# A two-layer network on one core: v and y by groups in DRAM, ScalarE's queue for v, and the side work of the last gate product dealt out over its rows

## The chip, the core and the metric

One core of a Trainium2 chip runs the whole program in one launch. The metric is the device time of an execution in microseconds (us), as the median of several executions.

## What is computed

Two layers over 512 tokens and a model width of 2048, in fp32. Layer 0 (forgetting attention beside an RWKV-7 mix) is untouched by the change. Layer 1 and the end that both layers share are, cut to what matters:

```python
def chunked_spatial_gating(u, v, ln_g, ln_b, w_s, b_s):      # chunks of 128 tokens, 16 groups of 128 channels
    u = gelu(u)
    v = layer_norm(gelu(v), ln_g, ln_b)
    vc = v.reshape(B, T // 128, 128, 16, 128)
    mixed = einsum('gts,bnsgc->bntgc', w_s * causal, vc) + b_s.T[:, :, None]
    return u * mixed.reshape(B, T, 2048)

xn = rms_norm(h, norm_pre[1])
u, v, g = split(xn @ c_w_in, 3)                              # 2048 x 6144
oc = chunked_spatial_gating(u, v, c_ln_g, c_ln_b, c_w_s, c_b_s)
y = (oc * silu(g)) @ c_w_out                                 # 2048 x 2048
h = h + rms_norm(y, norm_post[1])
h = h + (p[1] @ ple_w_proj[1]) * sigmoid(h @ ple_w_gate[1])  # the last gate product, 2048 x 2048
```

## The kernel before

**Products.** Every fp32 product is made of three matmuls of halves: an operand is cast to a rounded high part (`hi`, by ScalarE) and the rest is its low part (`lo`, VectorE subtracts); then hi*hi, hi*lo and lo*hi are added in PSUM. Weights come by DMA into `raw` or `rq` buffers; `pieces` casts them to `whi` (L1352, ScalarE) and `wlo` (L1353, VectorE), with four buffers each.

**Seven products.** The two large products of the change, `xn @ c_w_in` and `h @ ple_w_gate`, are computed by the scheme of seven block products in place of eight (`seven`, matmuls at L1380 to L1382). The tokens are halved (256 and 256), the contraction is halved (channel tiles 0 to 7 and 8 to 15), and a pair of 512-column blocks is taken at a time. The left operands are *sets* of blocks: set 1 is the block of the first half and the first tokens (`A11`), set 2 the one of the second half (`x2`), set 4 the block of the second half and the later tokens (`set22`), and sets 5, 6, 3 and 7 are sums and differences of blocks (S1, S2, S4 and S3 in `sets`, at L1243, L1246, L1249 and L1252). Each block of a set is split into hi and lo by `finish` (L959 ScalarE, L960 VectorE). For some of the products the weights are differences too: GpSimd loads a second block on top of the first with an accumulating DMA (L1309), or VectorE adds (L1313). A product is 8 rows of 6 matmuls (128x128 by 128x512).

**Side work.** After each row `seven` calls `tick()`; `later(n, step)` hangs a step n rows ahead. The steps are written into the program at that row, and a scheduler then sets each engine's order from the program's order, dependencies and priorities. So the places in the code are a request, and the order of each engine is to be read from the engine's own list.

**Layer C (layer 1).** The columns of v come first: `vals` applies gelu and stores v in DRAM (`vd`, [128, 4, 2048]: token in chunk, chunk, channel). Then u and g follow by column pairs, the result staying in `u[n]`. `mix(g, at)` hangs four steps for each of 16 groups around a row `at`: `load` at -11 (v of the group into buffer `sq`, L1467, w_s, L1468, and two rows of the layer norm spread over partitions, L1469 and L1470, into the buffers `rstdB` or `accq`; all four on SP's queue), `norm` at -7 (four activations of ScalarE, L1476, a mask and two multiply-adds of GpSimd, L1480 and L1481), `split` at 0 (w_s transposed, both cast) and `mul` at +3 (three matmuls, L1486, and VectorE's gating of u, L1492). The first half of the result y is stored (`yd2`, L1543, on ScalarE's queue) and comes back on SP's queue at L1536 for its transposes, while the later column pairs are still computed.

**Last layer.** `post_norm` multiplies by `c_w_out`. Behind it TensorE does the small product `p @ ple_w_proj` as filler; ScalarE copies its results into `sg` (L1134) and SP stores them (`pd`, L1135). Then `update` adds the normed y to h on VectorE (L1143, L1144), first for the first 256 tokens (e = 0), later for the other half (e = 1). `A11` is split right behind its updates. `sets` then does, in one stretch of code: set 2, the updates of e = 1, and all sums. `flip(g, m)` transposes h back to token order (TensorE L1157), ScalarE copies it into `sg` (L1159) and stores it to `rd` (L1160); sixteen flips hang at rows 0 to 15, and set 4 at row 16. The gate product runs over its 14 block products; `fetch` brings `pd` and `rd` back on SP's queue (L1185, L1186) into spare buffers, and `emit` multiplies by the sigmoid, adds (L1189 to L1192) and stores the output (L1194).

Each kind of temporary buffer in the pool `wp` (`sg`, `sq`) has two buffers, so a third writer waits until the first has been read.

## Time and profile before

| | |
|---|---|
| timed, median of 2 runs | 2325.9 us (2325.39 to 2326.41) |
| the profiled execution | 2323.41 us, its span from first to last instruction 2321.7 us |
| TensorE (PE) busy | 2237.6 us, 96% of the span |
| TensorE weight loads (PEld), beside it | 79% |
| VectorE (DVE) / ScalarE (ACT) / GpSimd (POOL) | 64% / 53% / 12% |
| mean granted TensorE clock | 0.987 of full speed |
| DMA | mean 134 GB/s over the span |
| layer C, from about 1480 us on | to about 1920 us, TensorE busy 406.61 of 440 us |
| its output product | to about 2090 us, busy 170.00 of 170 us |
| filler, first rows of the last gate product | to about 2182 us, busy 67.31 of 92 us |
| the rest of it, to the end | busy 126.86 of 139 us |

How rows of the trace are read below. A window row gives its start and end, its length, TensorE's busy time with the number of matmuls, the granted clock, the mean share of 16 DMA engines and GB/s. An instruction row gives its start, its length, engine, line, operation, what it writes <- reads and its shape, how often it follows at once (x4), and in brackets the idle time ahead of it and what ended it. "SPq" and "ACTq" are the queues by which SP and ScalarE issue transfers. A group row (a line, an operation, a shape, a count) gives busy time and mean ns of one, then the idle time ahead of its instructions. A row with KB gives the count of transfers, the size of one and the median time from issue to landing. A wait row gives the sum, the count and the longest.

### The profile page before, as it was taken

How to read it: one execution, taken by the hardware profiler on the slowest of the kernel's cores; microseconds unless marked ns; L12 is line 12 of the kernel's file. 1: busy time of each engine (PE TensorE's matmuls, PEld its weight loads, DVE VectorE, ACT ScalarE, POOL GpSimd, SP SyncE). 2: the span in 40 equal slices, each digit the busy share in tenths (PEclk: the TensorE clock that was granted, in tenths of full speed). 3: DMA queues.
4: the chain of work that ended last, by engine and by line, in shares of the span. 5: the costliest groups of instructions: out<-in, count | busy, mean ns of one | idle time of the engine just before them, and what ended most of it. 6: DMA issues, size and time to landing. Idle time of an engine off the chain costs nothing.

```text
span 2321.7 us, 39023 instructions
## 1 busy us (share of the span) xinstructions
PE 2237.6 (96%) x14787; PEld 1823.7 (79%) x14787; DVE 1480.6 (64%) x2817; ACT 1229.2 (53%) x2510; POOL 284.8 (12%) x334
## 2 busy tenths in 40 slices
PE   9999999999999999999999999999979989996898
PEld 7878888888887888878888888887658768885676
DVE  8666657766535878852365469877766764228668
ACT  5455555555444777743354357565545643336544
POOL 2000101010100000001100011122330220010010
PEclk9999999999999999999999999999999989999899
DMA  6332223222335433352335345896576764335786
GB/s 229 89 85 77 67 72 88 72 79 61 96 96 170 124 100 105 84 162 92 109 112 164 118 136 158 210 237 165 139 178 180 178 178 135 100 100 163 240 226 196
DMA packets 298969, 311.58 MB, mean 134 GB/s; under 512 B 14701, under 2 KB 198158, under 8 KB 297758
## 3 DMA queue, kind: packets, MB, share of 16 engines
q1 hardware_dynamic: 275614, 265.06, 37.7%
q0 software_dynamic: 17408, 33.56, 8.5%
q10 hardware_dynamic: 5760, 10.49, 1.2%
q8 instruction: 116, 1.90, 0.3%
q14 instruction: 71, 0.58, 0.1%
HBM read 274.15 MB, written 34.90 MB: 133 GB/s over the span
## 4 chain that ended last, share of the span: by engine, by line
PE 76%; DMA 9%; DVE 9%; ACT 3%; issue 2%; SPq 0%; POOL 0%; ACTq 0%; DVEq 0%
PE mm L195 11%; PE mm L197 11%; PE mm L196 11%; PE mm L982 6%; PE mm L983 6%; PE mm L981 6%; PE mm L1381 5%; PE mm L1382 5%; PE mm L1380 5%; DVE wlo L1353 3%; DMA sq<-vd 2%; DMA rq<-in_ple_w_gate_dram 2%; PE tm L533 1%; DMA rq<-in_c_w_in_dram 1%; PE tm L554 1%
## 5 line engine op out<-in xcount | busy, mean ns | idle before, releaser
L181 DVE TENSOR_TENSOR wlo<-raw,whi 128x512 fp32r<-128x512 f32 x464 | 331.8, 722 | 423.3 <-ACT whi L179 383.8
L179 ACT CAST whi<-raw 128x512 fp32r<-128x512 f32 x464 | 287.3, 620 | 455.9 <-PE mm L982 222.4
L196 PE MATMUL mm<-xl,whi 128*128 128x512 f32 x1088 | 426.9, 392 | 0.0
L195 PE MATMUL mm<-xh,whi 128*128 128x512 f32 x1008 | 418.1, 415 | 0.0
L197 PE MATMUL mm<-xh,wlo 128*128 128x512 f32 x1008 | 398.0, 395 | 0.0
L1353 DVE TENSOR_TENSOR wlo<-rq,whi 128x512 fp32r<-128x512 f32 x336 | 240.9, 728 | 121.2 <-ACT whi L1352 120.8
L1352 ACT CAST whi<-rq 128x512 fp32r<-128x512 f32 x336 | 206.2, 620 | 150.0 <-PE mm L1382 86.6
L196 PEld LDWEIGHTS mm<-xl,whi 128*128 128x128 f32 x1088 | 205.2, 189 | 33.6
L197 PEld LDWEIGHTS mm<-xh,wlo 128*128 128x128 f32 x1008 | 189.2, 188 | 41.8
L195 PEld LDWEIGHTS mm<-xh,whi 128*128 128x128 f32 x1008 | 189.8, 188 | 33.8
L981 PE MATMUL mm<-yl,whi 128*128 128x512 f32 x336 | 130.9, 390 | 0.0
L983 PE MATMUL mm<-yl,wlo 128*128 128x512 f32 x336 | 130.7, 389 | 0.0
L1380 PE MATMUL mm<-whi,yh 128*128 128x512 f32 x256 | 103.2, 403 | 14.8 <-ACT whi L1352 14.8
L1424 POOL TENSOR_TENSOR accq<-accq,sq 128x512 f32<-128x512 f32 x42 | 56.8, 1353 | 476.5 <-ACT sq L1422 475.4
L982 PE MATMUL mm<-xl,whi 128*128 128x512 f32 x288 | 112.0, 389 | 0.0
L1381 PE MATMUL mm<-wlo,yh 128*128 128x512 f32 x256 | 103.2, 403 | 4.2 <-DVE wlo L1353 4.2
L1381 PE MATMUL mm<-wlo,yl 128*128 128x512 f32 x256 | 101.4, 396 | 4.9 <-DVE wlo L1353 4.9
L1381 PE MATMUL mm<-wlo,xl 128*128 128x512 f32 x256 | 101.6, 397 | 4.3 <-DVE wlo L1353 4.0
L1380 PE MATMUL mm<-whi,yl 128*128 128x512 f32 x256 | 101.2, 395 | 3.5 <-ACT whi L1352 2.8
L1382 PE MATMUL mm<-whi,yh 128*128 128x512 f32 x256 | 101.9, 398 | 0.0
L1380 PE MATMUL mm<-whi,xl 128*128 128x512 f32 x256 | 101.1, 395 | 0.0
L1382 PE MATMUL mm<-whi,yl 128*128 128x512 f32 x256 | 100.7, 393 | 0.0
(486 smaller groups left out, 4701.3 us busy)
## 6 DMA issues: line engine op xcount, KB each, us to landing
raw<-in_ab_w_in_dram SPq DMA_DIRECT2D x128, 512.0 KB, 3.9
rq<-in_c_w_in_dram SPq DMA_DIRECT2D x75, 512.0 KB, 6.9
rq<-in_c_w_in_dram POOLq DMA_DIRECT2D x38, 512.0 KB, 8.5
raw<-in_ple_w_gate_dram SPq DMA_DIRECT2D x36, 512.0 KB, 3.8
rq<-in_ple_w_gate_dram SPq DMA_DIRECT2D x36, 512.0 KB, 5.1
raw<-in_ab_w_out_dram SPq DMA_DIRECT2D x32, 512.0 KB, 3.7
raw<-in_c_w_out_dram SPq DMA_DIRECT2D x32, 512.0 KB, 3.8
raw<-in_c_w_in_dram SPq DMA_DIRECT2D x25, 512.0 KB, 6.2
```

The source lines that it names most:

```text
L179: nc.scalar.copy(hi[:, : m * n], src)
L181: self.weng.tensor_tensor(lo[:, : m * n], src, f(hi[:, : m * n]), ALU.subtract)
L195: nc.tensor.matmul(acc, hi, xhi[k], start=(k == 0), stop=False)
L196: nc.tensor.matmul(acc, hi, xlo[k], start=False, stop=False)
L197: nc.tensor.matmul(acc, lo, xhi[k], start=False, stop=(k == nk - 1))
L981: nc.tensor.matmul(accs[j], hi[:, js], xhi[k], start=(k == 0), stop=False)
L982: nc.tensor.matmul(accs[j], hi[:, js], xlo[k], start=False, stop=False)
L983: nc.tensor.matmul(accs[j], lo[:, js], xhi[k], start=False, stop=(k == nk - 1))
L1353: nc.vector.tensor_tensor(lo, src, f(hi), ALU.subtract)
L1380: nc.tensor.matmul(acc[m], xh, hi, start=(first and r == 0), stop=False, **more)
L1381: nc.tensor.matmul(acc[m], xh, lo, start=False, stop=False, **more)
L1382: nc.tensor.matmul(acc[m], xl, hi, start=False, stop=(r == 7), **more)
```

## The change

v and the first half of y are kept in DRAM by groups of 128 channels, so that what a group needs lies together: `vd` is [128, 16, 4, 128] and `yd2` [128, 8, 4, 128]. Stores are scattered into rows of 512 bytes, loads read 2 KB in one piece per partition. The four loads of a group's `load` go out by ScalarE's queue instead of SP's; `norm` hangs at -5 instead of -7 and `mul` at +4 instead of +3. y is loaded eight rows instead of five ahead of its transposes, which hang one to three rows later. The stores of `pd` go out by ScalarE's queue, from `sg` and `sq` in turn.

In the last layer the stretch `sets` becomes closures of one q each (`sums`), and these and the flips are hung at rows: flips of the first tokens at 1 to 8, the updates of e = 1 with set 5 at 2, 6, 10 and 14, sets 6 and 3 at 19 to 28 (which form the difference `less` a second time), flips of the later tokens at 20 to 34, set 7 at 37 to 40, set 4 at 42. The first fetches go into the eight `yh` buffers that set 7 takes over later, and from row 46 on into the former spares. For layer 1's other call of the sums the order is the same as before, since it runs them at once.

```diff
-            self.vd, self.pd, self.rd = (self.t(dp, [P, 4, D], n) for n in ("vd", "pd", "rd"))
-            self.yd2 = self.t(dp, [P, 4, 2 * T], "yd2")
+            self.pd, self.rd = (self.t(dp, [P, 4, D], n) for n in ("pd", "rd"))
+            self.vd, self.yd2 = (self.t(dp, [P, c, 4, P], n) for n, c in (("vd", KT), ("yd2", 8)))
...
                 for m in range(4):
-                    pj = self.t(wp, [P, T], "sg")
+                    pj = self.t(wp, [P, T], ("sg", "sq")[m % 2])
                     nc.scalar.copy(pj, accs[m])
-                    nc.sync.dma_start(self.pd[:, m, g * T : (g + 1) * T], pj)
+                    nc.scalar.dma_start(self.pd[:, m, g * T : (g + 1) * T], pj)
...
+        sets, x2, less, s1, s24, s3 = self.sums(H, wp)
+        sets[1] = A11
+        for q in range(4):
+            x2(q)
+        spare = [[], []]
         def late(q):
             update(q, 1)
             update(q + 4, 1)
-        sets = self.sets(A11, H, ps, wp, None, False, late)
+            s1(q)
...
+        def early_spare():
+            for j in range(8):
+                spare[j % 2].append(self.slot("yh", j, F32))
+        def late_spare():
             for j in range(2):
                 tl = self.t(self.xp, [P, 4, T], f"xh{2 + j}")
-                spare.append([tl[:, q, :] for q in range(4)])
-        for k, (g, m) in enumerate((g, m) for g in (2, 0, 3, 1) for m in range(4)):
-            self.later(k, lambda g=g, m=m: flip(g, m))
-        self.later(16, rest)
+                spare[j][:] = [tl[:, q, :] for q in range(4)]
+        def x22():
+            sets[4] = self.set22(H, wp, False)
+        steps = [(1 + k, lambda g=g, m=m: flip(g, m)) for k, (g, m) in enumerate((g, m) for g in (2, 0, 3, 1) for m in (0, 1))]
+        steps += [(2 + 4 * q, lambda q=q: late(q)) for q in range(4)]
+        steps += [(16, early_spare)]
+        steps += [(19 + 3 * q, lambda q=q: s24(q, less(q))) for q in range(4)]
+        steps += [(20 + 2 * k, lambda g=g, m=m: flip(g, m)) for k, (g, m) in enumerate((g, m) for g in (2, 0, 3, 1) for m in (2, 3))]
+        steps += [(37 + q, lambda q=q: s3(q)) for q in range(4)]
+        steps += [(42, x22), (46, late_spare)]
+        for n, step in steps:
+            self.later(n, step)
...
+    def sums(self, xs, wp):
...
+        def x2(q):
+            self.part(s[2], q, xs[q + 4, 0])
+        def less(q):
+            t = self.tmp(wp, "sg")
             nc.vector.tensor_tensor(t, xs[q, 1], xs[q + 4, 1], ALU.subtract)
...
+        def s1(q):
+            t = less(q)
+            self.part(s[5], q, t)
+            return t
+        def s24(q, t):
+            u = self.tmp(wp, "sq")
             nc.vector.scalar_tensor_tensor(u, t, -1.0, xs[q, 0], ALU.mult, ALU.subtract)
+            self.part(s[6], q, u)
+            t = self.tmp(wp, "sg")
             nc.vector.scalar_tensor_tensor(t, u, -1.0, xs[q + 4, 0], ALU.mult, ALU.subtract)
+            self.part(s[3], q, t)
+        def s3(q):
+            t = self.tmp(wp, "sq")
             nc.vector.tensor_tensor(t, xs[q, 0], xs[q, 1], ALU.add)
...
-            nc.scalar.dma_start(self.vd[:, m, n * T : (n + 1) * T], dst)
+            nc.scalar.dma_start(self.vd[:, 4 * n : 4 * n + 4, m, :], dst.rearrange("p (g c) -> p g c", c=P))
...
-                nc.sync.dma_start(vn, self.vd[:, :, gs])
-                nc.sync.dma_start(own["ws"], i["c_w_s"][0, g])
-                nc.sync.dma_start(own["bc"][:, 0, :], i["c_ln_g"][0, gs].partition_broadcast(P))
-                nc.sync.dma_start(own["bc"][:, 1, :], i["c_ln_b"][0, gs].partition_broadcast(P))
+                nc.scalar.dma_start(vn, self.vd[:, g])
+                nc.scalar.dma_start(own["ws"], i["c_w_s"][0, g])
+                nc.scalar.dma_start(own["bc"][:, 0, :], i["c_ln_g"][0, gs].partition_broadcast(P))
+                nc.scalar.dma_start(own["bc"][:, 1, :], i["c_ln_b"][0, gs].partition_broadcast(P))
...
-            for n, step in ((-11, load), (-7, norm), (0, split), (3, mul)):
+            for n, step in ((-11, load), (-5, norm), (0, split), (4, mul)):
...
-                nc.sync.dma_start(y, self.yd2[:, :, n * P : (n + 1) * P])
-            self.later(at - 5, load)
+                nc.sync.dma_start(y, self.yd2[:, n])
+            self.later(at - 8, load)
...
-                nc.scalar.dma_start(self.yd2[:, m, n * T : (n + 1) * T], u[n][:, m, :])
+                nc.scalar.dma_start(self.yd2[:, 4 * n : 4 * n + 4, m, :], u[n][:, m, :].rearrange("p (g c) -> p g c", c=P))
...
-                    early(n, (14, 18, 22, 26, 31, 35, 39, 43)[n])
+                    early(n, (17, 21, 25, 29, 32, 36, 40, 44)[n])
```

Line numbers move with the change: L1140 and L1141 are the copy and the store of `pd`, L1149 and L1150 the update, L1163 to L1166 a flip, L1268, L1278, L1281 and L1286 the sums, L1384 and L1385 whi and wlo, L1499 to L1502 the four loads of a group, L1508 its norm, L1520 and L1523 the casts of its `split`, L1575 the store of `yd2`.

**VectorE, at the start of the last gate product.** Before, the updates of a block of h (`yh_4263`, `yh_4269`, ...: L1143, L1144) and the low parts of the first set (`xh_4492`, L960) alternate; `wlo` at L181 belongs to the products ahead.

```order
L1143 TENSOR_TENSOR xl_4260_20528<-xl_4260_20528,rstdB_12776 128x512
L1143 TENSOR_TENSOR xl_4266_20544<-xl_4266_20544,rstdB_12776 128x512
L1144 TENSOR_TENSOR yh_4263_20537<-yh_4263_20537,xl_4260_20528 128x512
L1144 TENSOR_TENSOR yh_4269_20553<-yh_4269_20553,xl_4266_20544 128x512
L181 TENSOR_TENSOR wlo_21621<-raw_21602,whi_21620 128x512
L960 TENSOR_TENSOR xh_4492_21699<-yh_4263_20537,xh_4491_21698 128x512
L960 TENSOR_TENSOR xh_4492_21699<-yh_4269_20553,xh_4491_21698 128x512
L1143 TENSOR_TENSOR xl_4316_20836<-xl_4316_20836,rstdB_12776 128x512
L1143 TENSOR_TENSOR xl_4322_20852<-xl_4322_20852,rstdB_12776 128x512
L181 TENSOR_TENSOR wlo_21655<-raw_21652,whi_21654 128x512
L1144 TENSOR_TENSOR yh_4319_20845<-yh_4319_20845,xl_4316_20836 128x512
L1144 TENSOR_TENSOR yh_4325_20861<-yh_4325_20861,xl_4322_20852 128x512
```

In the change's order the last rows ahead of those low parts are these: updates of the later tokens (`yh_4320`, `yh_4398`, `xh_4411` and so on).

```order
L1149 TENSOR_TENSOR xl_4317_20838<-xl_4317_20838,rstdB_12776 128x512
L1149 TENSOR_TENSOR yh_4398_21262<-yh_4398_21262,rstdB_12776 128x512
L1385 TENSOR_TENSOR wlo_21833<-rq_4537_21812,whi_21832 128x512
L1150 TENSOR_TENSOR yh_4320_20847<-yh_4320_20847,xl_4317_20838 128x512
L1150 TENSOR_TENSOR xh_4411_21338<-xh_4411_21338,yh_4398_21262 128x512
L1149 TENSOR_TENSOR xl_4323_20854<-xl_4323_20854,rstdB_12776 128x512
L1149 TENSOR_TENSOR yh_4425_21415<-yh_4425_21415,rstdB_12776 128x512
L1150 TENSOR_TENSOR yh_4326_20863<-yh_4326_20863,xl_4323_20854 128x512
L1150 TENSOR_TENSOR xh_4411_21338<-xh_4411_21338,yh_4425_21415 128x512
L960 TENSOR_TENSOR xh_4492_21699<-yh_4263_20537,xh_4491_21698 128x512
L960 TENSOR_TENSOR xh_4492_21699<-yh_4269_20553,xh_4491_21698 128x512
L960 TENSOR_TENSOR xh_4492_21699<-yh_4319_20845,xh_4491_21698 128x512
```

The first low part of the first set (`xh_4492<-yh_4263`) stood behind the second pair of updates; it stands behind all 32 update instructions, those of the later tokens included.

**ScalarE, at the same place.** Before: the copies of the filler's results (L1134, into `sg`) between the casts of weights (L179) and of the first set (`xh_4491`, L959).

```order
L1134 COPY sg_21531<-mm_21493 128x512
L1134 COPY sg_21534<-mm_21494 128x512
L179 CAST whi_21620<-raw_21602 128x512
L959 CAST xh_4491_21698<-yh_4263_20537 128x512
L959 CAST xh_4491_21698<-yh_4269_20553 128x512
L1134 COPY sg_21537<-mm_21495 128x512
L1134 COPY sg_21540<-mm_21496 128x512
L179 CAST whi_21654<-raw_21652 128x512
L959 CAST xh_4491_21698<-yh_4319_20845 128x512
L179 CAST whi_21670<-raw_21652 128x512
```

In the change (the copies at L1140 into `sg` and `sq`, their stores to `pd` at L1141 as ScalarE's own rows):

```order
L1384 CAST whi_21832<-rq_4537_21812 128x512
L1141 DMA pd_101<-sq_21645 128x512
L1141 DMA pd_101<-sg_21686 128x512
L1140 COPY sq_21689<-mm_21649 128x512
L1140 COPY sg_21692<-mm_21650 128x512
L1141 DMA pd_101<-sq_21689 128x512
L1141 DMA pd_101<-sg_21692 128x512
L1140 COPY sq_21695<-mm_21651 128x512
L959 CAST xh_4491_21698<-yh_4263_20537 128x512
L1141 DMA pd_101<-sq_21695 128x512
L959 CAST xh_4491_21698<-yh_4269_20553 128x512
```

The casts of the first set stand behind all sixteen copies, and between the copies stand the stores that were on SP's queue.

**The loads of a group in layer C.** Before, SP issues them among the loads of weights (`rq`, L1305); the name `vd_101` is v in DRAM, `accq` and `rstdB` hold w_s and the two rows of the norm.

```order
L1470 DMA accq_18104<-in_c_ln_b_dram 128x128
L1305 DMA rq_3792_18394<-in_c_w_in_dram 128x2x512
L1467 DMA sq_18105<-vd_101 128x4x128
L1305 DMA rq_3798_18422<-in_c_w_in_dram 128x2x512
L1467 DMA sq_18205<-vd_101 128x4x128
L1468 DMA rstdB_12776<-in_c_w_s_dram 128x128
L1305 DMA rq_3803_18445<-in_c_w_in_dram 128x2x512
L1469 DMA rstdB_12776<-in_c_ln_g_dram 128x128
L1470 DMA rstdB_12776<-in_c_ln_b_dram 128x128
L1305 DMA rq_3833_18584<-in_c_w_in_dram 128x2x512
L1467 DMA sq_18297<-vd_101 128x4x128
```

In the change they are rows of ScalarE, here the piece from one load of v to the next (`sq_18105` is that group's v, `whi` the casts of weights):

```order
L1499 DMA sq_18105<-vd_103 128x512
L1523 CAST sg_18171<-sq_18005 128x512
L1384 CAST whi_18213<-rq_3664_17827 128x512
L1575 DMA yd_36_104<-xh_3540_17257 128x4x128
L1384 CAST whi_18223<-rq_3664_17827 128x512
L1520 CAST w_3743_18168<-mm_18166 128x128
L1508 ACTIVATE sq_18105<-sq_18105,nb_15727,rv_15726 128x128 x2
L1384 CAST whi_18240<-rq_3731_18115 128x512
L1508 ACTIVATE sq_18105<-sq_18105,nb_15727,rv_15726 128x128 x2
L1384 CAST whi_18250<-rq_3731_18115 128x512
L1499 DMA sq_18205<-vd_103 128x512
```

The load of v stands five rows, two of them casts of whi, ahead of its norm on the engine that issues it, and no longer behind a load of weights on SP's queue.

More of the change, by code (lines that the diff above doesn't have):

```diff
@@ L1226, in part, with pair @@
         self.finish(src, s[0][q], s[1][q])
-    def sets(self, A11, xs, ps, wp, place, copy, late=lambda q: None):
-        nc = self.nc
-        pair = lambda k, j: self.slot(k, j).rearrange("p (a t) -> p a t", a=2)
-        tmp = lambda tag: self.t(wp, [P, T], tag).rearrange("p (a t) -> p a t", a=2)
-        new = lambda k, o: [[pair(k, o + 4 * e + q) for q in range(4)] for e in range(2)]
-        A12, S1, S2, S4 = new("yl", 0), new("yl", 8), new("xl", 0), new("xl", 8)
-        S3 = [[], []]
-        for q in range(4):
-            self.part(A12, q, xs[q + 4, 0])
-        for q in range(4):
-            late(q)
-        for q in range(4):
-            t = tmp("sg")
-            nc.vector.tensor_tensor(t, xs[q, 1], xs[q + 4, 1], ALU.subtract)
-            self.part(S1, q, t)
-            u = tmp("sq")
+    def pair(self, k, n):
+        return self.slot(k, n).rearrange("p (a t) -> p a t", a=2)
@@ L1253, in sets, with set22 @@
             for e in range(2):
-                S3[e].append(pair("yh", 2 * q + e))
-            self.part(S3, q, t)
-        sets = {1: A11, 2: A12, 3: S4, 5: S1, 6: S2, 7: S3}
-        if place is not None:
-            sets[4] = self.set22(xs, wp, place, copy)
-        return sets
-    def set22(self, xs, wp, place, copy):
+                s[7][e].append(self.pair("yh", 2 * q + e))
+            self.part(s[7], q, t)
+        return s, x2, less, s1, s24, s3
+    def set22(self, xs, wp, copy):
```

26 lines of the change are left out of this document (15 added, 11 removed).

## The prediction

> **What bounds the kernel now.** I read the page first, for the engine that is never done, then TensorE's waits, then windows of 4 to 6 us around the longest waits, then the single instructions there.
>
> ```profile
> PE 2237.6 (96%) x14787; PEld 1823.7 (79%) x14787; DVE 1480.6 (64%) x2817; ACT 1229.2 (53%) x2510; POOL 284.8 (12%) x334
> PE mm L1157 <- ACT sg L1159: 21.5, 5, 18.6
> PE mm L1380 <- ACT whi L1352: 19.4, 7, 7.6
> ACT sq L1476 <- DMA sq<-vd: 53.9, 10, 12.3
> ```
>
> TensorE is busy 96% of the span, so what can be won is its gaps, and two lines of its wait table (total, times, longest) name the long ones; the third row is ScalarE's wait for v. The longest single gap, 18.6 us, is a transpose of h that waits for a copy by ScalarE; two of 7 us are matmuls that wait for whi, ScalarE's cast of the weights. A gap also lowers the granted clock, so I price it in windows (length, PE busy, granted clock, DMA share): lost time is length less busy time by clock.
>
> ```profile
> 1684.00:1690.00 6.00, 4.45 (x21) 1.00 1.10 249
> 1690.00:1695.00 5.00, 0.00 (x0) 0.79 0.91 181
> 1695.00:1700.00 5.00, 3.66 (x8) 0.50 0.40 121
> 1700.00:1704.00 4.00, 4.00 (x11) 0.61 0.60 181
> 1876.00:1880.00 4.00, 1.44 (x7) 1.00 1.07 208
> 1880.00:1885.00 5.00, 0.00 (x0) 0.56 0.31 59
> 1885.00:1890.00 5.00, 4.23 (x8) 0.50 0.33 107
> 1890.00:1896.00 6.00, 6.00 (x21) 0.64 0.57 173
> 2132.00:2150.00 18.00, 0.39 (x2) 0.63 0.35 59
> 2150.00:2156.00 6.00, 3.08 (x12) 0.50 0.34 131
> 2156.00:2160.00 4.00, 3.98 (x9) 0.50 0.83 258
> ```
>
> Stall A (1684 to 1704) loses 1.6 + 5.0 + 3.2 + 1.6 = 11.3 us. Stall B (1876 to 1896) loses 2.6 + 5.0 + 2.9 + 2.2 = 12.6 us. Stall C (2132 to 2160) loses 17.6 + 4.5 + 2.0 = 24.1 us. In each, some 4 to 5 us is the half clock after the gap, about 8 us long. It sets in late: A's gap began at 1688.45 (1695.23 - 6.78), and a mean of 0.79 over 1690 to 1695 puts the step at 1692.9; B's began at 1877.4, and 0.56 over 1880 to 1885 puts it at 1880.6; so 3.2 to 4.5 us after the start. A and B lie in the gate products of layer C, C in the last product. What ends them:
>
> ```profile
> 1681.49 0.38 SPq L1305 DMA_DIRECT2D rq<-in_c_w_in_dram  x1
> 1682.74 0.53 SPq L1467 DMA_DIRECT2D sq<-vd  x1
> 1694.17 0.49 ACT L1476 ACTIVATE sq<-sq,nb,rv 128x128 f32<-128x128 f32 x1 [11.70 <-DMA sq<-vd]
> 1695.23 0.79 PE L1380 MATMUL mm<-whi,yh 128*128 128x512 f32 x1 [6.78 <-ACT whi L1352]
> 1725.90 0.88 ACT L1476 ACTIVATE sq<-sq,nb,rv 128x128 f32<-128x128 f32 x2 [5.23 <-DMA sq<-vd]
> 1727.33 0.51 PE L1380 MATMUL mm<-whi,xh 128*128 128x512 f32 x1 [1.80 <-ACT whi L1352]
> 1885.05 0.79 PE L1380 MATMUL mm<-whi,yh 128*128 128x512 f32 x1 [7.61 <-ACT whi L1352]
> 2150.95 1.11 PE L1157 MATMUL mm<-ident,yh 128*128 128x128 f32 x4 [18.56 <-ACT sg L1159]
> ```
>
> In A the load of a group of v is issued at 1682.74, right behind a weight load; ScalarE reaches that group's norm and stands 11.70 us for it, with the casts of whi queued behind; TensorE lives for 4.9 us (11.70 less 6.78) on weights that are cast already. At 1725.90 the same wait of 5.23 us costs TensorE 1.80, a lead of 3.4. So a wait of ScalarE below about 3.5 us costs nothing, and one above costs what exceeds it. The ten waits for v are the one mechanism behind A, B and some 4 us of smaller gaps (1.8 of them at 1727.33).
>
> **The loads of v by ScalarE's queue.** The four loads of a group (v, w_s and the two rows of the norm) leave SP's queue, 64 in all, and stand in ScalarE's order. The issue itself costs ScalarE next to nothing:
>
> ```profile
> 1669.50 0.34 ACTq L1543 DMA_DIRECT2D yd<-xh  x1
> 1669.61 0.48 ACT L1476 ACTIVATE sq<-sq,nb,rv 128x128 f32<-128x128 f32 x1
> ```
>
> An issue of 0.34 us runs while the next activation is already at work. Were it serial, 64 x 0.34 = 22 us would be added to an engine that is 53% busy, still beside TensorE. The sixteen stores of v and the eight of y become rows of 512 B, and their issue may go from 0.33 us to the 0.53 that the load in such pieces took at 1682.74; 24 x 0.2 = 5 us beside other work; if that cover were gone, 5 us.
>
> What counts is how fast v lands. Around A the bytes in flight are this load (0.26 MB), the weight load ahead (0.52) and about four accumulating loads of GpSimd (2.1), 2.9 MB; at the 249 GB/s of the first window that is 11.6 us, the 11.7 that was waited. On a queue of its own the load need not wait for the weight load ahead of it in SP's queue, and against the accumulating loads it gets a share. The nearest rows, with 256 KB each:
>
> ```profile
> sq<-vd SPq DMA_DIRECT2D x16, 256.0 KB, 3.4
> vd<-comb ACTq DMA_DIRECT2D x8, 256.0 KB, 6.7
> ```
>
> Median landing was 3.4 us for the load on SP, and 6.7 us for stores of the same size on ScalarE's queue in the crowded stretch before. I bound the new landing by 2 x 3.4 and 6.7 above, 3.4 below, and take 5. In the order of the change a load stands two to five casts of weights ahead of its norm; a row of six matmuls is 1.4 us (six starts 0.23 apart, as 2114.87 and 2115.10 further down), so 2.7 to 7 us pass in between. ScalarE then waits 0 to 4 us, about its lead: hardly a gap. The norm also comes two rows later, which adds cover, and leaves five rows (7 us) before the split for four activations (4 x 0.48 by the row at 1669.61) and two multiplies on GpSimd:
>
> ```profile
> 1640.31 1.41 POOL L1480 TENSOR_TENSOR sq<-sq,accq 128x512 f32<-128x512 f32 x1 [2.75 <-ACT sq L1476]
> ```
>
> That is 1.9 + 2.8 us, so it fits.
>
> The Trainium skill, DMA: Bandwidth & Descriptors, section Issuing engines are not separate DMA queues, speaks against this: all queues end on the same 16 engines, and several issuers save only the issue time. By it alone the 11.7 us stay. The same page's Queues, rings and completion order has each engine go round the queues packet by packet, by which a small load on an idle queue passes the weight backlog. The trace of before cannot separate the two, since all loads of v were on SP's queue; I let them stand as rivals.
>
> Against this stand the new waits. What ScalarE's issues must wait for is what SP's did:
>
> ```profile
> SPq L1467 <- DVE sg L1492: 22.0, 14, 7.0
> SPq L1468 <- PE mm L1486: 17.7, 6, 7.8
> SPq L1469 <- POOL sq L1480: 31.4, 7, 9.6
> SPq L1470 <- POOL sq L1481: 7.7, 6, 1.3
> ```
>
> 79 us in 16 groups. SP ran ahead and stood there with nothing but weight loads behind it; ScalarE arrives later: its rows for the two norm vectors stand one or two casts behind the norm whose multiplies (1.4 us each on GpSimd) they wait for, so I expect 1 to 2 us each, within the lead. Queued behind such a wait are whi, and with it VectorE's wlo and TensorE. Bounds for this whole part: 0 to 28 us won (A + B + 4) less the new waits; I take 20, leaving 8 us for waits that exceed the lead. SP, freed of 79 us of standing, can issue weights earlier; no price is put on it.
>
> **The sums and transposes dealt out.** Before, all sums of h stood on VectorE ahead of the second product, and the transposes of the second half of h waited behind them through the buffer sg. In C nothing but VectorE works:
>
> ```profile
> 2097.63 1.29 DVE L1143 TENSOR_TENSOR xl<-xl,rstdB 128x512 f32<-128x512 f32 x2
> 2114.87 0.39 PE L238 MATMUL mm<-whi,comb 128*128 128x512 f32 x1
> 2115.10 0.39 PE L1380 MATMUL mm<-whi,xh 128*128 128x512 f32 x1
> 2138.16 0.68 DVE L1243 TENSOR_TENSOR sg<-yh,xh 128x512 f32<-128x512 f32 x1
> 2142.97 0.68 DVE L1243 TENSOR_TENSOR sg<-yh,xh 128x512 f32<-128x512 f32 x1
> L1134 ACT COPY sg<-mm 128x512 f32<-128x512 f32 x16 | 9.2, 587 | 5.7 <-DMA pd<-sg 5.6
> L1313 DVE TENSOR_TENSOR rq<-rq,rq 128x1024 f32<-128x1024 f32 x31 | 37.9, 1222 | 11.8 <-DMA rq<-in_ple_w_gate_dram 9.5 <-DMA rq<-in_c_w_in_dram 2.1
> ```
>
> Between the two rows of L1243 stand eight VectorE instructions in 4.81 us, 0.60 each. Dealt out over 48 rows of matmuls (48 x 1.4, with 16 x 4 transposes at 0.23, = 82 us), the 80 instructions of the sums (four more than before, since the difference is formed twice), 48 wlo, and 8 adds of 1.2 us with some 8 for the results make 136 x 0.60 + 10 = 92 us from 2097.6 on, against TensorE's 82 us from 2115.1: VectorE ends near 2190 and TensorE near 2197, so TensorE need not wait for the sums as a whole and the 24.1 us of C go. The cover is thin: if VectorE is the later one by a few us in the products with adds, that is lost again.
>
> What is late next is the start. In the changed order VectorE does all sixteen updates of the second half of h (0.60 each) before it forms the low parts of the first set: 39 instructions stand between the first update and the first of these low parts, so it comes at 2097.6 + 39 x 0.60 + 0.7 = 2121.8. Before, the first product began at 2115.10, right behind the side product. Its third matmul needs that low part. ScalarE reaches the casts of this set no sooner than about 2116 to 2120, since sixteen copies (0.59) with sixteen issues (0.34), each behind its own copy, and six casts (0.6) now stand ahead of them: 16 x 0.93 + 3.6 = 18.5 us from 2097.6 is 2116.1, and waits for the landing of earlier stores come on top. TensorE therefore stands from 2115.1 to 2121.8, with two matmuls in between: 6.3 us. In the windows the clock fell 3 to 4.5 us after a gap began, and came back 8 us after its end, so a half clock for about 8 us, 4 us, follows (0 if the two matmuls keep the clock up). The Trainium skill, TensorE: Matmul & The Clock Gate, Part 1, has 3.4 us for either step; by it the price would be about half, 1.7 us. The windows show a longer return, and I keep 4. After it VectorE's 92 us and TensorE's 82 us plus these 10 end about together.
>
> Part sum: 24.1 - 6.3 - 4 = 14 us won, with bounds of 24 (no first gap) and 8 (late sums). The stores of pd on ScalarE's queue with four buffers instead of two cost nothing else there, since TensorE works on the side product; uncovered they are the 18.5 us counted above. The first four fetches go to eight slots that were free, so that the reuse of slots at the end is relaxed:
>
> ```profile
> 2256.00:2264.00 8.00, 4.99 (x16) 0.79 0.96 308
> ```
>
> This is the largest loss there, 8 - 4.99 x 0.79 = 4.1 us, with the DMA engines full. It can go, or, with the same transfers pressed into less time, double: I take 0, bounds 4 won and 4 lost. The loads of y move three rows earlier into a stretch without gaps: 0.
>
> **Sum.** The profiled execution took 2323.4 us (span 2321.7). 2323.4 - 20 - 14 = 2289.4. The timed median, 2325.9, lies 2.5 above it, so the forecast is 2292, 1.5% faster.
>
> **Rivals.** (1) The 16 DMA engines are what is short, not the place in SP's queue: then v lands as late as before, stalls A and B stay, and only the last layer gains: 2325.9 - 14 = 2312. For it speaks that 2.9 MB at 249 GB/s explain the 11.7 us with no queue in it; against it, that a store on ScalarE's own queue landed in 6.7 us while the engines were as busy. The Trainium skill's sentence on issuing engines (DMA: Bandwidth & Descriptors, named above) would give this time. (2) ScalarE stands where SP stood, and the change is slower: 79 us in 16 groups is 4.9 us a group, with a landing of 3.4 us 8.3 in all; less the lead of 3.7 that leaves 4.6 us of gap a group, 74 us. 2325.9 - 14 - 28 + 74 = 2358. It becomes a loss when ScalarE stands more than 6.3 us a group (3.7 + 42 / 16). Against it: ScalarE is not ahead of those it waits for, as SP was. (3) The first-set gap does not come, or without loss of clock, the waits for v vanish wholly, and the end gains too: 2325.9 - 28 - 24 - 4 = 2270. For it speaks that ten waits with a median landing of 3.4 us need little to vanish; against it, that the order of the 39 instructions is fixed and VectorE has no faster rate in the trace.
>
> **How the numbers follow.** Forecast (2280 to 2305) 0.58; rival 1 0.17; rival 2 0.07; rival 3 0.18. Range 2266 to 2322: from rival 3, 4 us below its time, to rival 1 with 10 us for the bounds of the end (4) and of late sums (6); rival 2 is left out. About 2% (2279 and 2372) is what a measurement of this kernel can tell from no change. Below 2279 lies rival 3 with a little of the forecast, 0.2; above 2372 the upper part of rival 2, 0.03; the rest 0.77.
>
> **What would show it.** Right: no TensorE gap over 3 us in the gate products, waits of ScalarE for v below 5 us, landing of v near 5; in the last product one gap of 5 to 7 us at the start of its first row, ended by the low part of the first set, and none of 18. Wrong: landings of 10 us and more on ScalarE's queue (rival 1); waits of ScalarE's issues for GpSimd or VectorE of 4 us and more in most groups (rival 2); or a first row that follows the side product at once (rival 3).

## The result and the profile after

The change takes 2296.59 us (median of 2 runs, 2295.81 to 2297.37) against 2325.9: ratio 0.9874, interval 0.9832 to 0.9916, 1.3% faster. The forecast was 2292, in a range of 2266 to 2322. The profiled execution took 2295.81 us (span 2294.0), 27.6 us less than that of before.

The line of busy times on the page of the change:

```profile
PE 2230.5 (97%) x14787; PEld 1823.1 (79%) x14787; DVE 1485.0 (65%) x2821; ACT 1226.0 (53%) x2510; POOL 289.8 (13%) x334
```

Its table of waits, of TensorE over the whole span and of ScalarE from 1500 to 1900 us (engine, line, what it waited for: total, times, longest):

```profile
PE mm L1413 <- DVE wlo L1385: 29.1, 20, 6.6
PE mm L1412 <- ACT xh L959: 6.2, 1, 6.2
ACT sq L1508 <- DMA sq<-vd: 7.9, 4, 3.8
ACT whi L1384 <- POOL sq L1512: 6.7, 3, 3.0
ACT whi L1384 <- PE mm L1550: 5.7, 1, 5.7
ACT whi L1384 <- issue: 3.6, 3, 3.2
```

The view of the one line that loads v: how long its issues stood at a semaphore (ns, min/median/max, first and last start), and its landings:

```profile
L1499 ACTq EVENT_SEMAPHORE  x12: 17/17/5475, 1508.4 to 1856.2; - x12
DMA to landing us min/median/max: 2.8/3.0/3.1
```

The trace holds the landing of only three of these sixteen loads (before, of five). For others a wait shows when v came; the latest is this one, 5.8 us after its issue:

```profile
1714.66 0.34 ACTq L1499 DMA_DIRECT2D sq<-vd  x1
1720.45 0.88 ACT L1508 ACTIVATE sq<-sq,nb,rv 128x128 f32<-128x128 f32 x2 [3.80 <-DMA sq<-vd]
```

ScalarE's waits for v fell from 53.9 us to 7.9, the longest from 12.3 to 3.8. The waits of TensorE for whi (19.4 us before) and for the transposes' copies (21.5) are gone from the head of the table. It waits for wlo, VectorE's part, 29.1 us against 15.0. The rows on L1512, L1550 and "issue" are ScalarE standing at a load that must wait for its buffer: the new wait that was priced against the gain, 5.7 us at the longest. (That row names a matmul, but what ScalarE stood at is the issue of L1499 that waited 5.475 us from 1856.2 on.)

Where the output product behind layer C began (the matmuls of L981 that read xh: count, ns min/median/max, first and last start), before:

```profile
L981 PE MATMUL mm<-xh,whi x48: 389/389/477, 1914.2 to 2014.7; 128*128 128x512 f32 x48
```

and with the change:

```profile
L981 PE MATMUL mm<-xh,whi x48: 389/389/478, 1894.1 to 1994.6; 128*128 128x512 f32 x48
```

20.1 us were won ahead of this point, and 27.7 - 20.1 = 7.6 us behind it. The last layer in windows of 4 us (first row to last: the gap at its start, a second one, one near the end):

```profile
2096.00:2100.00 4.00, 0.00 (x0) 0.00 (x0) 3.82 (x7) 2.19 (x4) 0.00 (x0) 1.00 0.95 322
2100.00:2104.00 4.00, 2.66 (x6) 2.01 (x7) 4.00 (x8) 3.70 (x7) 0.00 (x0) 0.53 0.94 314
2104.00:2108.00 4.00, 4.00 (x17) 3.31 (x16) 2.85 (x5) 2.62 (x5) 0.00 (x0) 0.61 0.15 56
2124.00:2128.00 4.00, 1.32 (x5) 1.09 (x6) 2.67 (x5) 2.02 (x5) 1.08 (x1) 0.95 0.32 123
2128.00:2132.00 4.00, 4.00 (x13) 3.15 (x12) 2.07 (x4) 1.91 (x4) 2.51 (x3) 0.63 0.88 172
2224.00:2228.00 4.00, 1.17 (x6) 0.63 (x4) 0.00 (x0) 0.62 (x1) 0.00 (x0) 1.00 1.08 256
2228.00:2232.00 4.00, 0.20 (x1) 0.20 (x2) 2.08 (x3) 0.00 (x0) 0.00 (x0) 0.75 1.06 376
2232.00:2236.00 4.00, 4.00 (x10) 3.13 (x11) 4.00 (x7) 1.67 (x3) 1.38 (x2) 0.50 1.07 336
```

Lost time is length less TensorE busy time by clock, as in the prediction: 9.0 us at the start (with 0.85 from 2092 to 2096), 4.2 at 2124 to 2132, 8.7 at 2224 to 2236. The 24.1 us of stall C are gone. The instructions that ended these gaps, and what stood ahead on ScalarE and VectorE:

```profile
2094.76 0.39 PE L238 MATMUL mm<-whi,comb 128*128 128x512 f32 x1
2101.34 0.80 PE L1412 MATMUL mm<-whi,xh 128*128 128x512 f32 x1 [6.19 <-ACT xh L959]
2077.52 1.29 DVE L1149 TENSOR_TENSOR xl<-xl,rstdB 128x512 f32<-128x512 f32 x2
2101.32 2.50 DVE L960 TENSOR_TENSOR xh<-yh,xh 128x512 fp32r<-128x512 f32 x4
2100.67 0.62 ACT L959 CAST xh<-yh 128x512 fp32r<-128x512 f32 x1
2126.68 0.50 PE L1413 MATMUL mm<-wlo,xh 128*128 128x512 f32 x1 [2.73 <-DVE wlo L1385]
2125.32 0.69 DVE L1268 TENSOR_TENSOR sg<-yh,xh 128x512 f32<-128x512 f32 x1 [3.10 <-DMA rd<-sg]
2231.80 0.79 PE L1413 MATMUL mm<-wlo,yl 128*128 128x512 f32 x1 [6.62 <-DVE wlo L1385]
2229.91 1.23 DVE L1345 TENSOR_TENSOR rq<-rq,rq 128x1024 f32<-128x1024 f32 x1 [9.02 <-DMA rq<-in_ple_w_gate_dram]
```

From the first update to the first low part VectorE took 2101.32 - 2077.52 = 23.80 us, and ScalarE's first cast of the set came only 0.65 us ahead of that: both were late together. TensorE's wait ended with the cast. It came 2100.67 - 2077.52 = 23.15 us after the first update, since four of the copies ahead of it stood for the landing of earlier stores (2.34, 1.13, 1.12 and 0.82 us). In the second gap a sum (L1268) waits for a buffer `sg` until a transposed copy of h has landed in DRAM, with wlo queued behind. In the third, VectorE waits 9.02 us for weights, with the DMA engines full (share 1.06 to 1.08).

### The profile page after: what moved, and what is told of

It reads as the page before. It is cut to its first block, busy times and chain, and to the rows that moved or that the text cites. A ratio compares the mean times of both kernels' runs of the same rounds, so it can differ in the third digit from the quotient of the medians.

```text
span 2294.0 us, 38975 instructions
## 1 busy us (share of the span) xinstructions
PE 2230.5 (97%) x14787; PEld 1823.1 (79%) x14787; DVE 1485.0 (65%) x2821; ACT 1226.0 (53%) x2510; POOL 289.8 (13%) x334
## 4 chain that ended last, share of the span: by engine, by line
PE 78%; DVE 9%; DMA 7%; ACT 3%; issue 3%; SPq 0%; POOL 0%; ACTq 0%; DVEq 0%; POOLq 0%
PE mm L195 11%; PE mm L197 11%; PE mm L196 11%; PE mm L981 6%; PE mm L983 6%; PE mm L982 6%; PE mm L1413 5%; PE mm L1414 5%; PE mm L1412 5%; DVE wlo L1385 3%; DMA rq<-in_ple_w_gate_dram 2%; PE tm L533 1%; DMA rd<-sg 1%; DVE rq L1345 1%; PE tm L554 1%
## 5 line engine op out<-in xcount | busy, mean ns | idle before, releaser
L181 DVE TENSOR_TENSOR wlo<-raw,whi 128x512 fp32r<-128x512 f32 x464 | 331.7, 722 | 423.5 <-ACT whi L179 384.7
L179 ACT CAST whi<-raw 128x512 fp32r<-128x512 f32 x464 | 287.2, 620 | 459.1 <-PE mm L982 227.8
L1384 ACT CAST whi<-rq 128x512 fp32r<-128x512 f32 x336 | 206.7, 621 | 167.9 <-PE mm L1414 91.4
L1385 DVE TENSOR_TENSOR wlo<-rq,whi 128x512 fp32r<-128x512 f32 x336 | 241.6, 730 | 77.7 <-ACT whi L1384 77.2
L197 PEld LDWEIGHTS mm<-xh,wlo 128*128 128x128 f32 x1008 | 189.4, 188 | 41.7
L981 PE MATMUL mm<-yl,whi 128*128 128x512 f32 x336 | 130.9, 390 | 0.0
L1413 PE MATMUL mm<-wlo,xl 128*128 128x512 f32 x256 | 103.0, 402 | 11.7 <-DVE wlo L1385 11.6
L1412 PE MATMUL mm<-whi,xl 128*128 128x512 f32 x256 | 102.7, 401 | 0.0
L1414 PE MATMUL mm<-whi,xl 128*128 128x512 f32 x256 | 102.1, 399 | 0.0
L1414 PE MATMUL mm<-whi,yh 128*128 128x512 f32 x256 | 99.9, 390 | 1.1 <-DVE yh L960 1.1
```

The lines of the kernel that those rows point to most:

```text
L179: nc.scalar.copy(hi[:, : m * n], src)
L181: self.weng.tensor_tensor(lo[:, : m * n], src, f(hi[:, : m * n]), ALU.subtract)
L197: nc.tensor.matmul(acc, lo, xhi[k], start=False, stop=(k == nk - 1))
L981: nc.tensor.matmul(accs[j], hi[:, js], xhi[k], start=(k == 0), stop=False)
L1385: nc.vector.tensor_tensor(lo, src, f(hi), ALU.subtract)
L1412: nc.tensor.matmul(acc[m], xh, hi, start=(first and r == 0), stop=False, **more)
```

## Experiments

Each ratio is to runs of the kernel before that were timed beside it on the same chip (their medians 2322 to 2324 us). The runs lie on several chips, so between kernels the ratios compare better than the medians. For the change itself the ratio is that of the result, from two runs of each.

**The two parts apart.** `mix_only` is the kernel before with the edits of `vd`, `yd2`, `mix` and `early`; `last_only` is the change without them.

> The kernel before with layer C's part of the change alone (v and y by groups, the four loads of a group on ScalarE's queue, norm at -5, mul at +4, y earlier); the last layer as before. In the traces of before and of the change the output product behind layer C began at 1914.2 and at 1894.1 us, 20 us apart. If the two parts are independent, this kernel takes 2325.9 - 20 = 2306 us, and its last layer shows the 18.6 us wait of the transpose again. Rival: the parts help each other (less traffic in one, an earlier start in the other), then it stays above 2312 and the last layer's part carries more than the 8 us left over.

> The change with layer C's part undone, so the last layer's part alone. By the traces from the start of the output product to the end: 407.5 us before, 399.9 with the change, 7.6 us won, so 2325.9 - 7.6 = 2318 us. The forecast had 14 us for this part, 2312 us. A gap of about 6 us in front of the first product, one of 5 to 7 us near the end, none of 18.

`mix_only`: 2303.83 us, ratio 0.9923 (0.9903 to 0.9943). `last_only`: 2313.45 us, ratio 0.9964 (0.9951 to 0.9977). By medians 18.9 and 9.2 us, 28.1 together, against 29.3 for the whole: the parts add, within the intervals. In the last layer `mix_only` has the old gap:

```profile
2129.45 1.12 PE L1157 MATMUL mm<-ident,yh 128*128 128x128 f32 x4 [18.56 <-ACT sg L1159]
```

and `last_only` the new ones:

```profile
2117.46 0.80 PE L1412 MATMUL mm<-whi,xh 128*128 128x512 f32 x1 [6.58 <-ACT xh L959]
2248.69 0.79 PE L1413 MATMUL mm<-wlo,yl 128*128 128x512 f32 x1 [6.61 <-DVE wlo L1385]
```

The rival that the parts help each other falls.

**Layer C: queue, layout, or two numbers.** Three edits can make v less late. Six kernels, all with the new last layer, hold each alone or in a pair (in the three with one edit alone the loads of y stand at their old rows).

```diff
 loads_on_sp, layout_only, timing_only (the four loads of a group)
-                nc.scalar.dma_start(...)
+                nc.sync.dma_start(...)
 old_layout, queue_only, timing_only (v in DRAM; in the latter two also y)
-self.vd[:, 4 * n : 4 * n + 4, m, :] ... self.vd[:, g]
+self.vd[:, m, n * T : (n + 1) * T] ... self.vd[:, :, gs]
 norm7, layout_only, queue_only
-            for n, step in ((-11, load), (-5, norm), (0, split), (4, mul)):
+            for n, step in ((-11, load), (-7, norm), (0, split), (3, mul)):
```

> The change, with the four loads of a group issued by SP again (layout, norm at -5 and all else stay). Theory, the place in SP's queue behind weight loads is what made v late: the long landings return (over 10 us at the worst, against 3.1 with the change), ScalarE waits some 54 us less 2.8 for each of ten waits for v, about 25 us, and the time goes to 2308 to 2317 us. Rival, the scattered rows of 512 bytes made it late: landings stay near 3 us and the time within 3 us of 2296.6.

> The change, with v in DRAM in the old layout (loads scattered into rows of 512 bytes, stores in rows of 2 KB), issued by ScalarE as in the change; y stays by groups. Theory, the queue is what matters: landing of v 3 to 5 us, ScalarE's waits for v below 15 us in all, time within 3 us of 2296.6. Rival, the layout matters: landings of up to 12 us return, with the time at 2308 to 2317 us.

> The change, with norm back at -7 and mul at +3 (queue and layout as in the change). With the loads back on SP the time had risen by only 4 us, so the queue cannot be all of layer C's 19 us. Theory, the two rows that the norm comes later (2 x 1.4 us) carry most of it: ScalarE's waits for v rise from 7.9 us to 25 or more, and the time by 8 to 12 us against the change's 2296, to 2304 to 2308 us. Rival, a landing of 3 us on ScalarE's queue is enough by itself, since four rows (5.5 us) still lie between load and norm: waits below 15 us, time within 3 us of 2296.

> The last layer's part of the change, and of layer C's part only norm at -5 and mul at +4: the loads are SP's, in the old layout. The kernel without these two numbers took 2313.5 us, with 51.8 us of waits for v. Theory, the delay carries most: ten to twelve waits lose 2.8 us each, some 20 to 25 us are left, and the time falls by 10 to 14 us to 2300 to 2304. Rival, queue and layout carry it: landings of 9 to 12 us stay, each long wait keeps all but 2.8 us, and the time falls by 5 us at most, to 2308 or more.

> The last layer's part of the change, and of layer C's part the queue alone: the four loads of a group are issued by ScalarE; the layout of v and y, norm at -7, mul at +3 and the loads of y are as before. Without the queue the same kernel took 2313.5 us, with 51.8 us of waits for v and a worst landing of 9.2 us. Theory, the queue alone does it: worst landing below 7.5 us, waits for v below 20 us, time 2295 to 2299 us. Rival, it takes one of the other two edits beside it: waits above 30 us and a time of 2302 to 2309 us.

> The last layer's part of the change, and of layer C's part the layout alone: v and y by groups, all loads of a group on SP's queue, norm at -7, mul at +3, the loads of y at their old rows. Neither edit alone was enough so far (none 2313.5, the two numbers alone 2309.0, the queue alone 2305.5), every pair was (2296 to 2301). If the layout is like the others, one cause among three: 2303 to 2308 us with 30 to 45 us of waits for v. Rival, with a late norm gone the landing alone decides: 2298 to 2301 us, as with the later norm beside it.

The waits and the start of the output product (the first matmul of L981 that reads xh) are those of the profiled execution.

| edits of layer C in the kernel | median us | ratio to before | ScalarE's wait for v (total, times, longest) | output product starts at |
|---|---|---|---|---|
| none (`last_only`) | 2313.45 | 0.9964 (0.9951 to 0.9977) | 51.8, 12, 11.7 | 1909.8 |
| numbers (`timing_only`) | 2309.01 | 0.9935 (0.9920 to 0.9950) | 41.7, 10, 10.5 | 1908.7 |
| queue (`queue_only`) | 2305.54 | 0.9924 (0.9907 to 0.9941) | 21.8, 6, 9.8 | 1903.9 |
| layout (`layout_only`) | 2303.07 | 0.9927 (0.9908 to 0.9946) | 45.8, 11, 9.2 | 1905.9 |
| layout, numbers (`loads_on_sp`) | 2300.75 | 0.9908 (0.9890 to 0.9925) | 27.5, 9, 5.2 | 1899.1 |
| queue, numbers (`old_layout`) | 2296.23 | 0.9896 (0.9874 to 0.9918) | 10.5, 6, 4.7 | 1897.0 |
| queue, layout (`norm7`) | 2295.86 | 0.9878 (0.9862 to 0.9894) | 13.6, 5, 5.0 | 1894.3 |
| all three (the change) | 2296.59 | 0.9874 (0.9832 to 0.9916) | 7.9, 4, 3.8 | 1894.1 |

No edit alone brings the 17 us between the first row and the last; by medians each brings 4 to 10, by the start of the output product 1 to 6. The profiled execution of `layout_only` took 2309.04 us, 6 us more than its median, so its waits may be on the high side. By the times the queue with either of the others brings all of it, and then the third adds nothing that can be measured; by the start of the output product the queue with the numbers is 2.9 us short of all three. With the loads on SP the median rose by 4 us, a rise inside the intervals, between the theory (2308 us and more) and its rival (within 3 us); layout and later norm still hold the longest wait at 5.2 us. That the two numbers carry most fell with `norm7` and `timing_only`. That the queue alone does it fell with the time of `queue_only`; its waits of 21.8 us lie between the 20 of the theory and the 30 of the rival. There this is seen:

```profile
1861.69 0.53 ACTq L1499 DMA_DIRECT2D sq<-vd  x1
1873.42 0.49 ACT L1508 ACTIVATE sq<-sq,nb,rv 128x128 f32<-128x128 f32 x1 [9.77 <-DMA sq<-vd]
1874.47 0.80 PE L1412 MATMUL mm<-whi,yh 128*128 128x512 f32 x1 [6.42 <-ACT whi L1384]
```

and in windows of the same stretch:

```profile
1864.00:1868.00 4.00, 4.00 (x21) 3.04 (x19) 1.03 (x2) 0.00 (x0) 1.09 (x1) 1.00 1.02 207
1868.00:1872.00 4.00, 0.04 (x1) 0.00 (x0) 0.00 (x0) 0.00 (x0) 0.00 (x0) 1.00 1.10 212
```

This load on ScalarE's own queue still held the norm for 11.7 us after its issue, with the engines full (share 1.02 to 1.10): the first rival's mechanism, in one group. In `old_layout` the same load was issued at 1865.69 and held the norm only 1.15 us, 3.6 us after its issue, with a share of 0.67 from 1866 to 1870. That fits the crowding; why the engines were fuller in one of the two stays open.

**The gap ahead of the last product.** `a11_first` gives the first set a higher priority:

```diff
         for q in range(4):
-            update(q, 0)
-            self.part(A11, q, H[q, 0])
+            with self.tc.high_priority(2 * HP):
+                update(q, 0), self.part(A11, q, H[q, 0])
```

`less_sq` forms the first difference in `sq` in place of `sg` (also in layer 1's other call of the sums):

```diff
-            t = less(q)
+            t = less(q, "sq")
```

> The change, with the updates and the two halves of the first set given a higher priority, so that they stand ahead of the other updates on VectorE and ahead of most copies of the filler on ScalarE. If the 6.2 us gap in front of the last gate product and the half clock behind it (9.0 us together by windows) come from these two orders alone, it goes and the time falls by 6 to 9 us, to 2287 to 2290. Rival, the work only moves: the low weights wait behind the updates that are now late, a gap of the same size shows within the first product, and the time stays within 3 us of 2296.

> The change, with the first forming of the difference in the buffer sq in place of sg, which the copies of the flips use too. In the change VectorE stood 3.1 us ahead of L1268 until a store of sg had landed, with wlo queued behind it, and TensorE lost 4.2 us there (window 2124 to 2132). Theory, the shared buffer is the cause: this gap goes, 3 to 4 us faster, 2292 to 2293. Rival, VectorE is late in these rows anyway: a gap of 2 us or more remains there, time within 1.5 us of 2296.

`a11_first`: 2292.74 us (2292.06 to 2293.05), ratio 0.9864 (0.9847 to 0.9880), some 4 us better than the change. `less_sq`: 2296.06 us, ratio 0.9881 (0.9865 to 0.9897), no gain. The gaps of `a11_first`, with a buffer wait in the third row:

```profile
2112.42 1.14 PE L1163 MATMUL mm<-ident,yh 128*128 128x128 f32 x8 [2.34 <-ACT sg L1165]
2119.10 0.79 PE L1412 MATMUL mm<-whi,xh 128*128 128x512 f32 x1 [5.53 <-ACT sg L1165]
2122.56 0.58 ACT L1165 COPY sg<-mm 128x512 f32<-128x512 f32 x1 [2.48 <-DMA rd<-sg]
```

and of `less_sq`:

```profile
2132.92 0.69 DVE L1268 TENSOR_TENSOR sg<-yh,xh 128x512 f32<-128x512 f32 x1 [5.16 <-DMA rd<-sg]
2135.00 0.57 PE L1413 MATMUL mm<-wlo,yl 128*128 128x512 f32 x1 [3.87 <-DVE wlo L1385]
```

The gap of 6.2 us at the start went as expected, so the two orders together were its cause; this run moves both, and does not tell which was needed. But more than half of the gain was given back some 20 us later, at the buffers `sg`. They are shared by copies that must land in DRAM and by sums that need them for two instructions; moving one user (`less_sq`) moves the wait to the next. `less_sq` also has a new gap of 3.54 us at 2103.51, ended by VectorE's low part of the first set (L960); its cause stays open.

**Three causes at once.** `three` has, at three places: the norm's multiply and add (the "two multiplies" of the expectation) on VectorE; the priority of `a11_first` and buffers for the flips that no sum uses; the fetches on GpSimd's queue. `two` is the same with the fetches back on SP's.

```diff
-                nc.gpsimd.tensor_tensor(vn, vn, row(0), ALU.mult)
-                nc.gpsimd.tensor_tensor(vn, vn, row(1), ALU.add)
+                nc.vector.tensor_tensor(vn, vn, row(0), ALU.mult)
+                nc.vector.tensor_tensor(vn, vn, row(1), ALU.add)
...
+        turn = iter(range(16))
...
-            o = self.t(wp, [P, T], "sg")
+            k = next(turn)
+            o = self.rstdB if k > 7 and k % 2 else self.t(wp, [P, T], "accq", bufs=1) if k > 7 or k % 3 == 1 else self.t(wp, [P, T], "sq")
...
-                nc.sync.dma_start(pj[n, m], self.pd[:, m, n * T : (n + 1) * T])
-                nc.sync.dma_start(res[n, m], self.rd[:, m, n * T : (n + 1) * T])
+                nc.gpsimd.dma_start(pj[n, m], self.pd[:, m, n * T : (n + 1) * T])
+                nc.gpsimd.dma_start(res[n, m], self.rd[:, m, n * T : (n + 1) * T])
```

> The change with three edits at three places, each to be read at its own place. (1) Layer C: the two multiplies of a group's norm on VectorE in place of GpSimd. In the change VectorE's adds of weights took up to 3.4 us in place of 1.2 while GpSimd multiplied, and three gaps of TensorE of 2.2 to 3.1 us follow on them. Theory: these gaps go, the output product starts 8 to 12 us earlier than at 1894. Rival: 32 more instructions on VectorE (19 us) make wlo late elsewhere, start within 3 us of 1894. (2) Start of the last product: the first set at a higher priority, and the copies of the flips in buffers of their own (sq and accq, then accq and rstdB), so that no sum waits for the landing of a store. Theory: no gap of over 2 us in the first 60 us of the product, 9 to 12 us won against the change. Rival: VectorE itself is short there, gaps of 5 us in all stay. (3) The end: the fetches of pd and rd on GpSimd's queue, so that no weight load stands behind them on SP's. Theory: the gap of 6.6 us some 62 us from the end shrinks below 3. Rival, the 16 DMA engines are full there and it stays above 5. All theories together: 2296.5 - 10 - 10 - 5 = 2271 us; all rivals: 2293 to 2297.

> The kernel named three, with the fetches of pd and rd back on SP's queue; what is left of it are the multiplies of the norm on VectorE, the priority of the first set and the own buffers of the flips. In three the fetches' edit showed nothing at its place: the losses of the last 110 us were 13.3 us against 14 with the change, without the idle tail. If that holds, the time is 2279 to 2284 us. Rival: the gap near the end (3.75 us in three, 6.6 with the change) comes back in full with its half clock, then 2285 to 2288.

`three`: 2281.26 us, ratio 0.9823 (0.9808 to 0.9837), between the 2271 of all theories and the 2293 of all rivals. `two`: 2280.02 us, ratio 0.9819 (0.9801 to 0.9837), the fastest version, 1.8% under before. By place:

(1) The output product began at 1884.6 us in `three` and 1885.6 in `two`, 9 us earlier than with the change. Lines are two higher here; VectorE's adds of weights and wlo from 1480 to 1900 us, with the change (count, busy time and mean ns of one, idle before):

```profile
L1385 DVE TENSOR_TENSOR wlo<-rq,whi 128x512 fp32r<-128x512 f32 x196 | 146.8, 761 | 59.1 <-ACT whi L1384 59.0
L1345 DVE TENSOR_TENSOR rq<-rq,rq 128x1024 f32<-128x1024 f32 x20 | 30.8, 1538 | 2.3 <-DMA rq<-in_c_w_in_dram 2.0
```

and in `two`:

```profile
L1387 DVE TENSOR_TENSOR wlo<-rq,whi 128x512 fp32r<-128x512 f32 x196 | 133.1, 688 | 57.7 <-ACT whi L1386 57.2
L1347 DVE TENSOR_TENSOR rq<-rq,rq 128x1024 f32<-128x1024 f32 x20 | 24.3, 1221 | 8.5 <-DMA rq<-in_c_w_in_dram 8.4
```

The same work is faster by 13.7 and 6.5 us. Two of the three gaps named (2.2 and 2.6 us) went; the third, 3.1 us, is 3.3 in `two`, and there VectorE waits 5.08 us for weights. The edit also ends ScalarE's waits for GpSimd at the loads (6.7 us on L1512 with the change), so how much of the 9 us is VectorE's own speed is not shown.

(2) No gap at the start of the last product; one of 2.3 us further on in both, and one more of 2.3 in `three` alone. In the first 45 us of the product `two` loses 5.7 us and `three` 8.5, against 14.6 with the change: 9 and 6 us won; the expected 9 to 12 hold for `two`.

(3) The gap near the end is 3.75 us in `three`; in `two`, with the DMA engines full, it is

```profile
2216.23 0.79 PE L1415 MATMUL mm<-wlo,yl 128*128 128x512 f32 x1 [7.76 <-DVE wlo L1387]
```

with this window in it:

```profile
2210.00:2214.00 4.00, 0.00 (x0) 0.00 (x0) 0.00 (x0) 0.00 (x0) 0.00 (x0) 0.69 1.06 311
```

and the two times are the same within their spread. The gap shrinks with the other queue and no time is won, since other small gaps grew; so no run shows that the place in SP's queue costs time there. That the full DMA engines do is what the windows suggest; no run took transfers away there.

## Why the prediction was right, and where it was off

- **What bounds the kernel**: right. The gaps of TensorE were the price, and A, B and C are gone.
- **The loads of v**: 20 us were forecast, 20.1 measured by the start of the output product, 18.9 in `mix_only`. The mechanism held, the size came out right in part by luck, and the reason was too narrow. The sum was 28 us won less 8 for waits of ScalarE at its buffers that exceed the lead. Those cost next to nothing: TensorE's waits for whi in layer C fell from 19.4 us to 0.5. What was lost in their place is a term that the sum did not have, TensorE's waits for wlo in layer C (1480 to 1920 us), here before and with the change:

```profile
PE mm L1381 <- DVE wlo L1353: 8.7, 15, 1.7
PE mm L1413 <- DVE wlo L1385: 14.7, 12, 3.1
```

That is 6 us more, and the three longest gaps (2.4, 2.6 and 3.1 us) had the half clock behind them: two follow VectorE instructions that were slow beside GpSimd, one a wait of VectorE for weights, none ScalarE's standing. With the norm's arithmetic off GpSimd (`two`) these waits are 7.2 us.

- **Why v is in time**: the working let the place in the queue carry it and counted the later norm as added cover; the runs show three edits of which any pair with the queue is enough. That a wait of ScalarE below some 3.5 us costs nothing agrees with the change: its longest for v is 3.8 us, and no long gap of TensorE follows from v; even the 5.7 us at a buffer were followed by no gap that whi ended, so the lead can be longer than 3.5. The landing was taken as 5 us; three loads took 2.8 to 3.1, and the latest that a wait shows took 5.8. The rows that bounded it were thin: 3.4 us is the median of the five landings that the trace of before holds, 6.7 a single store of eight.
- **Rival 1** (only the engines are short) falls as the cause of the total, since the scattered loads on ScalarE's queue landed in time in `old_layout`; it holds for the one group in `queue_only`. What the Trainium skill says (DMA: Bandwidth & Descriptors, Issuing engines are not separate DMA queues) is therefore not refuted: with `queue_only` the trace agrees for that group, with 11.7 us at a share of 1.02 to 1.10, against 3.6 us at 0.67 in `old_layout`.
- **Rival 2** (ScalarE stands where SP stood): the waits exist, 6.7 + 5.7 + 3.6 us in the rows above, against SP's 79. TensorE lost nothing by them that its table shows. The 3.7 us of lead in this rival's price stand in no row; the rows give 3.4.
- **The first-set gap**: 6.3 us forecast, 6.19 measured. VectorE's 39 instructions took the 23.8 us of the working, but the gap ended with ScalarE's cast and not with the low part: with the waits for landings, which the working named without a price, the cast came 23.15 us after the first update in place of 18.5. That both came at the same time is chance. The half clock was set at 4 us and measured 9.0 - 6.2 = 2.8.
- **The last layer's sum**: 14 us forecast, 7.6 by the traces and 9.2 by `last_only` (6.4 of them, by its trace, behind the start of the output product). Two terms were mis-sized. "VectorE later by a few us" was named as thin cover and priced at nothing; it cost 4.2 us at 2126, and its cause was not VectorE's load but the buffer `sg` shared with copies on their way to DRAM, which the working priced for `pd` and not for the flips. The end was taken as 0 between 4 won and 4 lost; it lost 8.7 against 4.1 before, a little beyond the lower bound. The sum 14 - 4.2 - 4.6 + 1.2 (the clock) gives 6.4, close to the 7.6. (Stall C's first term is 18 - 0.39 x 0.63 = 17.8 by the working's own rule, not 17.6, which moves no conclusion.)
- **The signs it named**: no gap of 18 us is left and ScalarE's longest wait for v is below 5 us. Against them, the gate products of layer C keep one gap of TensorE over 3 us (3.14 us, restart 1684.97, ended by wlo).

The total came within 5 us because the larger part was right and the smaller part's error stayed inside the range.

## What to carry to other kernels

A load that is late for a known reader can be helped by its queue, by fewer and longer pieces, or by a later reader; try them in pairs before believing that one of them is the cause. When side work is dealt out over rows, count for each buffer who fills it and until when it is held: a buffer that waits for a landing in DRAM must not be shared with two-instruction temporaries, or each new place of the work makes a new wait.
